# Projecting q, k and v of all heads ahead of a latent attention, with q and k through memory, and spreading another attention's output products over its steps

## The chip, the cores and the metric

The kernel runs on one core of a Trainium2 chip. The metric is the time of one execution on the device in microseconds (us). A core has TensorE (PE in the profile; its weight loads are PEld), VectorE (DVE), ScalarE (ACT), GpSimd (POOL) and SyncE (SP, which issues nearly all DMAs here). They run side by side, each through a queue of its own, and wait for each other by semaphores. A "bank" below is a piece of PSUM, the memory that TensorE writes; it holds 128 rows of 512 floats.

## The reference

One decoder layer on x of 1024 tokens by 1024 features, all in float32:

```
h  = RMSNorm(x);  p = h @ w_in          # q, k, v of local attention | latents of q, kv | rope key | two gates
A  = local attention (8 heads of 64, 2 kv heads, window 128, learned sinks)
B  = latent attention: q = norm(q latent) @ w_uq, 8 heads of 64 + 32 rotary
                       k, v = norm(kv latent) @ w_ukv, 8 heads of 64 each
                       causal softmax over 1024 keys
y  = sigmoid(gate_a) * (A @ w_o_swa) + sigmoid(gate_b) * (B @ w_o_mla)
x  = x + y @ w_out;  x = x + SwiGLU(RMSNorm(x));  out = RMSNorm(x)
```

## The kernel before, in words

Every product is made in three matmuls: each operand is split into a high and a low part (`split`, L161 on: ScalarE copies the high part, VectorE subtracts it for the low one), and `mm3` (L169 on) adds high by high, high by low and low by high in a bank. So each tensor that TensorE is to read costs a ScalarE and a VectorE instruction first.

Order of the stages: the input projections, local attention with the gate products beside it (its outputs go to memory as oa_d), the latent attention, the output products of both attentions, the product with w_out, the feed-forward part, and the final norm. The change lies in the latent attention and in the output products.

*The latent attention.* The normalised latents are transposed into cq (three tiles) and ckv (two). Four helpers project them: `prod_rope(s)` (L1093) makes the rotary parts of q for all heads and 512 tokens and stores them to memory (qr_d), `prod_q(j, s)` (L1108) makes the other 64 rows of q of heads 2j and 2j+1, for 512 tokens, in one unit of 9 matmuls of 128x512, `prod_k(j, s)` (L1124) the same for k in 6, and `prod_v(b)` (L1132) v of all heads for 128 tokens in 6. prod_q and prod_k read their bank out in two halves of 64 rows, one per head, straight into that head's tiles qT and kT; the rotary rows of qT come from qr_d by DMA, and those of the three kT tiles, which are used in turn, are split three times from the transposed rope key.

Then come 64 steps (`for t in range(NT)`, L1301), eight per head, each a block of 128 queries, in the order 2, 3, 6, 7, 0, 1, 4, 5 (L1145). `scores(t)` (L1150) writes a block's scores to scb, one of two double banks; VectorE adds the mask and takes the maximum, ScalarE the exponential, GpSimd divides by the sum. `transposes(t)` (L1177) turns the block of probabilities p by TensorE into banks pTb, which ScalarE and VectorE split into pth and ptl. `pv(h, j)` (L1192) multiplies two blocks with v into half of a bank ob; when its second half is full, ScalarE and VectorE add up the parts. pTb, ob and the products oA come from the same four banks (`P1`, L153).

In step t stand: scores of step t+2; a pv that is due (4 steps behind its second block); in heads 0, 2, 4 a prod_q and in heads 1, 3, 5 a prod_k for the next heads, two of each; in the last eight steps a unit of `mix_a`; the transposes of step t-1; and splits of inputs for what follows.

*The output products.* `mix_a(dc, sh)` (L1248) is a unit of 12 matmuls: 128 columns of A @ w_o_swa for 512 tokens. `mix_b(dc)` (L1346) does the same for B in two units, multiplies both by the gates (loaded by `load_sig`, L1239) and adds. `early` (L1299) puts seven units of mix_a into the last eight steps; one follows behind, and the other eight are mixed with mix_b as listed in `steps` (L1361). The results of the first eight units wait in SBUF tiles ar.

*What sets the order.* Up to the end of local attention the order of PE and SP is the program's own (L329 to L1034). In the latent attention and in the output products it is a planner's: it takes, per engine, the first instruction in the program's order that it expects to be ready by its costs, and a tile waits for a free slot of its pool: 21 slots of 4 KB (`U`, L144), 17 of 8 KB (`V`, L147). Only ScalarE's copies under `held` (L159, L164) keep the program's order. What results is a fixed queue on each engine.

## Time and profile before

| what | value |
|---|---|
| median of 3 executions | 1357.09 us (1356.26 to 1359.11) |
| the profiled execution | 1357.54 us |
| its span in the trace | 1355.8 us, granted clock 0.999 |
| VectorE, ScalarE, GpSimd busy | 67%, 47%, 40% of the span |
| moved by DMA | 206.31 MB, mean 152 GB/s |
| first score matmul of the latent attention | 375.59 us |
| end of its last value product | 556.30 us |

The span starts with the first instruction of the trace and ends with the last. A row of a stretch of time gives its length and each engine's busy time in it, with the number of records. A row of a group or tile gives line, engine, operation, what is written and read, the count and the duration of one in ns (least, median, greatest, in a tile's rows). A row of a wait gives who waited for whom, the total in us, how often, and the longest.

### The profile page before, as it was taken

Reading aid. Unit: us, or ns where it says so; the run is one execution under the profiler, and the core shown is the slowest. Engines: PE = TensorE matmul, PEld = TensorE weight load, DVE = VectorE, ACT = ScalarE, POOL = GpSimd, SP = SyncE. Lnnn points to the kernel's source line nnn. Section 1 sums busy time; section 2 is a strip of 40 time slices with the busy share of each in tenths; the row PEclk is TensorE's granted clock in tenths of the full one; section 3 lists DMA queues with packets and bytes.
Section 4 is the critical chain, followed back from the end, with each engine's and each line's share of the span. In section 5 each row is a group of like instructions: output and inputs, shape, how many; then the busy total and the mean of one; then the engine's idle time right before and its main releaser. Section 6 shows DMA issues by size and latency. Waiting matters only on the chain.

```text
span 1355.8 us, 18965 instructions
## 1 busy us (share of the span) xinstructions
PE 1333.5 (98%) x6564; PEld 1116.0 (82%) x6564; DVE 913.6 (67%) x1493; ACT 641.7 (47%) x1301; POOL 548.9 (40%) x602
## 2 busy tenths in 40 slices
PE   9999999999999999999999999999999999999997
PEld 6899878878788878888887888888888888888886
DVE  7868767776777887585458866666656654664862
ACT  7434666675577777651336232322332332644343
POOL 2116546552254454200031565766665551022521
PEclk9999999999999999999999999999999999999999
DMA  9455322335410111671333353644435425996504
GB/s 372 151 188 163 116 87 82 119 111 190 132 37 16 40 48 32 233 254 42 121 158 140 124 179 143 222 178 179 152 136 179 163 86 184 379 383 242 171 10 146
DMA packets 79840, 206.31 MB, mean 152 GB/s; under 512 B 9089, under 2 KB 15745, under 8 KB 79489
## 3 DMA queue, kind: packets, MB, share of 16 engines
q1 hardware_dynamic: 78304, 202.74, 42.5%
q10 hardware_dynamic: 1440, 2.36, 0.5%
q8 instruction: 52, 0.85, 0.3%
q14 instruction: 44, 0.35, 0.1%
HBM read 143.34 MB, written 61.73 MB: 151 GB/s over the span
## 4 chain that ended last, share of the span: by engine, by line
PE 82%; DVE 7%; ACT 5%; issue 3%; POOL 2%; DMA 1%; ACTq 0%; POOLq 0%; DVEq 0%
PE fa L174 7%; PE fa L172 7%; PE fa L173 7%; PE fb L172 6%; PE fb L174 6%; PE fb L173 6%; PE fd L173 5%; PE fd L174 5%; PE fd L172 5%; PE xo L174 2%; PE xo L172 2%; PE xo L173 2%; DVE ptl L166 1%; DVE scb L1171 1%; ACT p L1172 1%
## 5 line engine op out<-in xcount | busy, mean ns | idle before, releaser
L166 DVE TENSOR_TENSOR wl<-wr,wl 128x512 fp32r<-128x512 f32 x150 | 151.0, 1031 | 72.7 <-ACT wl L163 72.4
L166 DVE TENSOR_TENSOR lrv<-lr,lrv 128x1024 fp32r<-128x1024 f32 x77 | 105.1, 1397 | 49.0 <-ACT lrv L163 46.4
L163 ACT CAST lrv<-lr 128x1024 fp32r<-128x1024 f32 x77 | 80.1, 1052 | 95.3 <-PE fd L174 68.8
L174 PE MATMUL fd<-lrv 128*128 128x512 f32 x308 | 119.9, 389 | 0.0
L172 PE MATMUL fd<-lrv 128*128 128x512 f32 x308 | 119.9, 389 | 0.0
L173 PE MATMUL fd<-lrv 128*128 128x512 f32 x308 | 119.9, 389 | 0.0
L177 POOL TENSOR_TENSOR wr<-wr,sm 128x512 f32<-128x512 f32 (+1 forms) x38 | 46.3, 1227 | 148.3 <-DVE wl L166 116.0
L163 ACT CAST wl<-wr 128x512 fp32r<-128x512 f32 x150 | 86.9, 623 | 2.0 <-DVE wr L826 1.7
L305 POOL TENSOR_SCALAR ms<-ss 128x1 f32<-128x1 f32 x32 | 8.8, 276 | 187.5 <-ACT xn L1578 111.2
L166 DVE TENSOR_TENSOR wl<-sm,wl 128x512 fp32r<-128x512 f32 x60 | 48.6, 835 | 46.6 <-ACT wl L163 46.5
L1173 POOL TENSOR_TENSOR denb<-denb,neg_one 128x1 f32<-128x1 f32 x64 | 36.8, 575 | 87.2 <-ACT p L1172 81.0
L172 PEld LDWEIGHTS fd<-lrv 128*128 128x128 f32 x308 | 57.9, 188 | 12.1
L174 PEld LDWEIGHTS fd<-lrv 128*128 128x128 f32 x308 | 57.9, 188 | 11.9
L173 PEld LDWEIGHTS fd<-lrv 128*128 128x128 f32 x308 | 57.9, 188 | 11.9
L1172 ACT ACTIVATE p<-scb,nmb 128x384 f32<-128x384 f32 (+3 forms) x64 | 47.6, 744 | 33.3 <-DVE nmb L1171 29.4
L166 DVE TENSOR_TENSOR ptl<-pTb,pth 128x512 fp32r<-128x512 f32 (+2 forms) x96 | 49.3, 550 | 19.9 <-ACT pth L163 19.5
L1470 ACT ACTIVATE act<-sm 128x512 f32<-128x512 f32 x11 | 7.0, 633 | 104.9 <-DVE sm L180 104.9
L1171 DVE CUSTOM_DVE_ANT_0 scb<-scb,mask 128x384 f32<-128x384 f32 (+3 forms) x64 | 48.2, 761 | 6.4 <-PE scb L1163 4.3
L1174 POOL TENSOR_SCALAR p<-p,denb 128x384 f32<-128x384 f32 (+3 forms) x64 | 49.5, 774 | 6.3
L1188 PE MATMUL pTb<-ident,p 128*128 128x128 f32 x288 | 44.8, 276 | 3.1 <-DVE ob L1222 1.4
L172 PE MATMUL fa<-t1h,wl 128*128 128x512 f32 x120 | 47.3, 394 | 0.4 <-ACT wl L163 0.4
L172 PE MATMUL fb<-t2h,wl 128*128 128x512 f32 x120 | 47.4, 395 | 0.0
(352 smaller groups left out, 4280.5 us busy)
## 6 DMA issues: line engine op xcount, KB each, us to landing
lr<-la_d SPq DMA_DIRECT2D x77, 256.0 KB, 5.4
wr<-in_w_gate_dram SPq DMA_DIRECT2D x22, 512.0 KB, 4.2
wr<-in_w_up_dram SPq DMA_DIRECT2D x22, 512.0 KB, 5.1
wd<-in_w_down_dram SPq DMA_DIRECT2D x22, 512.0 KB, 6.9
rb_d<-wd SPq DMA_DIRECT2D x22, 512.0 KB, 2.7
la_d<-sd SPq DMA_DIRECT2D x22, 512.0 KB, 5.3
lr<-rb_d SPq DMA_DIRECT2D x44, 256.0 KB, 5.4
lr<-in_w_down_dram SPq DMA_DIRECT2D x33, 256.0 KB, 5.4
```

Source lines behind the costliest of these rows:

```text
L163: i = nc.scalar.copy(hi, src)
L166: (eng or nc.vector).tensor_tensor(lo, src, hi.bitcast(F32), op=ALU.subtract)
L172: nc.tensor.matmul(ps, ah, bh, start=first and i == 0, stop=False, skip_group_check=go_on)
L173: nc.tensor.matmul(ps, ah, bl, start=False, stop=False, skip_group_check=go_on)
L174: nc.tensor.matmul(ps, al, bh, start=False, stop=last and i == n - 1, skip_group_check=go_on)
L177: eng.tensor_tensor(out, a, b, op=ALU.subtract)
L305: nc.gpsimd.tensor_scalar(ms, ss, 1.0 / width, EPS, op0=ALU.mult, op1=ALU.add)
L1171: nc.vector.tensor_tensor_reduce(s_, s_, m_, 1.0, -NEG, op0=ALU.add, op1=ALU.min, accum_out=nm)
L1172: nc.scalar.activation(p_, s_, AF.Exp, scale=-1.0, bias=nm, accum_out=den)
L1173: nc.gpsimd.tensor_tensor(den, den, neg_one[:, 0:1], op=ALU.pow)
L1174: nc.gpsimd.tensor_scalar(p[:, 0:w], p[:, 0:w], den, 0.0, op0=ALU.mult, op1=ALU.add)
L1188: nc.tensor.transpose(pp[:, i], p[:, blk(k0 + i)], ident)
```

## The change

Two new pairs of memory tensors take q and k of all heads (qn_d, kn_d), and a third the products A @ w_o_swa (ar_d).

Ahead of the steps all units of prod_rope, prod_q, prod_k and prod_v now stand in one loop over j, with the first two scores among the last of them. prod_q and prod_k read their bank out whole (128 rows) into a staging tile, which goes to memory; `load_k(h)` and `load_q(h)` bring a head's 64 rows back, three and two heads ahead. The rope key is split once, and two DMAs copy its rows to the other two kT tiles.

In the steps, heads 1 to 7 get four half units of mix_a each, of 6 matmuls: in the second and third step of a head the two halves of one unit, in the sixth and seventh those of another. So 14 units lie in the steps, and two follow. oa's loads stand ahead of the steps, its splits in the first eight. The transposes of step t stand in step t, and a pv is due after 3 steps. The w_o_swa weights are split in heads 0, 2, 4 and 6, into slots of V.

Behind the steps only mix_b is left. The product of mix_a comes back from ar_d with the two gates (`load_sigs`). The gate's product and one of the two additions are on GpSimd.

```
-    for nm, dp in (("oa", 0), ("oa", 1), ("oa", 2), ("ob", 0), ("ob", 1), ("oa", 3), ("ob", 2), ("ob", 3)):
-        plain((nm, dp), (w_o_swa if nm == "oa" else w_o_mla)[dp], (P, 4, 256))
+    for dp in range(4):
+        plain(("oa", dp), w_o_swa[dp], (P, 4, 256), True)
+    for dp in range(4):
+        plain(("ob", dp), w_o_mla[dp], (P, 4, 256))
...
-        for hi, lo in kT:
-            split(hi[64:QK, half(s)], lo[64:QK, half(s)], pr.rearrange("p b c -> p (b c)"))
+        split(kT[0][64:QK, 0, half(s)], kT[0][64:QK, 1, half(s)], pr.rearrange("p b c -> p (b c)"))
+    for i in range(1, 3):
+        nc.sync.dma_start(kT[i][64:QK].bitcast(F32), kT[0][64:QK].bitcast(F32))
...
     def prod_q(j, s):
...
-        for u in range(2):
-            hi, lo = (v[0:64, half(s)] for v in qT[2 * j + u])
-            p = ps[64 * u:64 * u + 64]
-            nc.scalar.activation(hi, p, AF.Copy, scale=-SC_B)
-            nc.vector.scalar_tensor_tensor(lo, p, -SC_B, hi.bitcast(F32), op0=ALU.mult, op1=ALU.subtract)
+        t = U("qns", F32R, (P, 2, 512))
+        nc.scalar.activation(t[:, 0], ps, AF.Copy, scale=-SC_B)
+        nc.vector.scalar_tensor_tensor(t[:, 1], ps, -SC_B, t[:, 0].bitcast(F32), op0=ALU.mult, op1=ALU.subtract)
+        nc.sync.dma_start(qn_d[j][:, :, half(s)], t.bitcast(F32))
...
     def prod_k(j, s):
...
-        for u in range(2):
-            hi, lo = kT[(2 * j + u) % 3]
-            split(hi[0:64, half(s)], lo[0:64, half(s)], ps[64 * u:64 * u + 64])
+        t = U("kns", F32R, (P, 2, 512))
+        split(t[:, 0], t[:, 1], ps)
+        nc.sync.dma_start(kn_d[j][:, :, half(s)], t.bitcast(F32))
...
+    def load_k(h):
+        nc.sync.dma_start(kT[h % 3][0:64].bitcast(F32), kn_d[h // 2, 64 * (h % 2):64 * (h % 2) + 64])
+
+    def load_q(h):
+        t = qT[h] = V("qT", F32R, (P, 2, S))
+        nc.sync.dma_start(t[0:64].bitcast(F32), qn_d[h // 2, 64 * (h % 2):64 * (h % 2) + 64])
+        for i in range(2):
+            nc.sync.dma_start(t[64 + 16 * i:80 + 16 * i].bitcast(F32), qr_d[i, 16 * h:16 * h + 16])
...
+    def mix_a(dc, sh, c0, n, ps=None):
...
+        mm3(ps, [((w[0][:, c, blk(dc % 2)], w[1][:, c, blk(dc % 2)]), oaT[(c, sh)]) for c in range(c0, c0 + n)],
+            c0 == 0, c0 + n == 4)
+        if c0 + n == 4:
+            nc.scalar.copy(ar[dc][:, half(sh)], oa_ps.pop((dc, sh)))
+            if sh == 1:
+                nc.sync.dma_start(ar_d[dc], ar.pop(dc))
...
+    def load_sigs(dc):
+        for i in (dc, 8 + dc):
+            load_sig(i)
+        ar[dc] = U("ar")
+        nc.sync.dma_start(ar[dc], ar_d[dc])
+
+    for j in range(4):
+        prod_k(j, 0)
+        prod_k(j, 1)
+        if j < 2:
+            prod_rope(j)
...
+        prod_q(j, 0)
+        if j == 1:
+            load_k(0)
+        if j == 2:
+            load_k(1)
+            load_q(0)
+        if j == 3:
+            load_k(2)
+            load_q(1)
+            psum_phase("psb", 2)
+            scores(0)
+        prod_q(j, 1)
+        prod_v(2 * j)
+        if j == 3:
+            scores(1)
+        prod_v(2 * j + 1)
+        if j == 1:
+            for g in range(2):
+                load_oa(g, 0)
+        if j == 3:
+            for g in range(2):
+                load_oa(g, 1)
+    st.load_to(st.index[("oa", 0)])
+    fill = {}
+    for i in range(16 - 2):
+        for c in range(2):
+            fill[NB * (i // 2 + 1) + 4 * (i % 2) + 1 + c] = (i // 2, i % 2, 2 * c)
...
-        if h + 1 < NH:
-            if n in (2, 4) and h % 2 == 0 and h + 2 < NH:
-                prod_q(h // 2 + 1, n // 2 - 1)
-            if n in (3, 5) and h % 2 == 1:
-                prod_k((h + 1) // 2, n // 2 - 1)
+        if n == 2 and h + 2 < NH:
+            load_q(h + 2)
+        if n == 6 and h + 3 < NH:
+            load_k(h + 3)
...
-            pvq.append((t + 4, hh, nn // 2))
+            pvq.append((t + 3, hh, nn // 2))
...
-        if e in early:
-            mix_a(*early[e], (PX if e >= 6 else P1)("oA"))
-        if t:
-            transposes(t - 1)
+        if t in fill:
+            dc, sh, c0 = fill[t]
+            mix_a(dc, sh, c0, 2, P1("oA") if c0 == 0 else None)
+        transposes(t)
...
+        if t < 8:
+            split_oa(t % 4 // 2, t // 4, t % 2)
+        if t == 4:
+            st.conv_to(st.index[("oa", 0)])
+        if n in (0, 4) and h in (2, 4, 6):
+            (st.load_to if n == 0 else st.conv_to)(st.index[("oa", h // 2)])
+        if e == 4:
+            load_sigs(0)
...
+    rest = [(i // 2, i % 2) for i in range(14, 16)]
+    mix_a(*rest[0], 0, 4, PX("oA"))
     for _, hp, j in pvq:
         pv(hp, j)
+    for r in rest[1:]:
+        mix_a(*r, 0, 4, PX("oA"))
...
     def mix_b(dc):
...
+        a_ = ar.pop(dc)
+        for sh in range(2):
+            nc.gpsimd.tensor_tensor(ga[:, half(sh)], a_[:, half(sh)], ga[:, half(sh)], op=ALU.mult)
...
+        for sh in range(2):
+            cs = half(sh)
+            add(ga[:, cs], ga[:, cs], gb[:, cs], (nc.vector, nc.gpsimd)[sh * (dc < 7)])
             split(*hT(dc, cs), ga[:, cs])
...
+    for dc in range(8):
+        if dc + 2 < 8:
+            load_sigs(dc + 2)
+        if dc % 2 == 0 and dc < 6:
+            st.load_to(st.index[("ob", dc // 2 + 1)])
+        if dc + 1 < 8:
+            sigmoids(dc + 1)
+        mix_b(dc)
+        if dc % 2 == 1 and dc < 6:
+            st.conv_to(st.index[("ob", dc // 2 + 1)])
+        if dc >= 4:
+            st.load_to(st.index[("out", 0, dc - 4)])
+        if dc >= 5:
+            st.conv_to(st.index[("out", 0, dc - 5)])
```

123 lines of the change are left out of this document (24 added, 99 removed).

## The prediction

> **What bounds the kernel now.** I read the page first, for the engine that sets the end, and then the latent attention by itself, because every part of the change lies in it or touches it.
>
> ```profile
> span 1355.8 us, 18965 instructions
> ...
> PE 1333.5 (98%) x6564; PEld 1116.0 (82%) x6564; DVE 913.6 (67%) x1493; ACT 641.7 (47%) x1301; POOL 548.9 (40%) x602
> ...
> PE 82%; DVE 7%; ACT 5%; issue 3%; POOL 2%; DMA 1%; ACTq 0%; POOLq 0%; DVEq 0%
> ```
>
> TensorE is busy 98% of the span and carries 82% of the chain of waits. The change moves matmuls without adding or dropping one, so it can only win time in which TensorE is not fed, and lose by starving it elsewhere. Busy time overstates feeding, because matmul records overlap. I therefore count starts. The next fence has the stretches of time from the first score matmul of each head to that of the next, the last stretch cut at 544; then the end of the attention, the projections ahead of it, and the output products behind it. Columns: length, then busy time (records) of PE, PEld, DVE, ACT, POOL, granted clock, DMA share, GB/s.
>
> ```profile
> 375.59:391.30 15.71, 15.15 (x87) 12.57 (x86) 11.80 (x25) 10.28 (x24) 8.35 (x14) 1.00 0.13 38
> 391.30:411.30 20.00, 19.12 (x127) 16.57 (x126) 17.00 (x37) 15.36 (x36) 10.05 (x15) 1.00 0.13 28
> 411.30:432.55 21.25, 20.37 (x133) 17.77 (x131) 16.26 (x36) 15.80 (x36) 11.69 (x18) 1.00 0.02 3
> 432.55:453.25 20.70, 19.25 (x125) 16.43 (x125) 15.80 (x35) 13.61 (x32) 9.11 (x15) 1.00 0.11 26
> 453.25:474.27 21.02, 20.10 (x133) 17.66 (x131) 16.65 (x36) 16.40 (x38) 11.48 (x18) 1.00 0.15 49
> 474.27:495.02 20.75, 19.38 (x126) 16.46 (x125) 17.42 (x38) 15.03 (x35) 9.72 (x15) 1.00 0.16 51
> 495.02:514.76 19.74, 18.14 (x118) 14.79 (x116) 17.90 (x36) 16.64 (x37) 10.85 (x16) 1.00 0.09 29
> 514.76:544.00 29.24, 29.04 (x169) 25.03 (x169) 19.53 (x41) 19.23 (x42) 13.09 (x18) 1.00 0.17 51
> 544.00:556.30 12.30, 12.30 (x76) 10.38 (x74) 5.58 (x9) 6.32 (x14) 1.46 (x2) 1.00 0.21 74
> ...
> 348.40:375.59 27.19, 26.46 (x114) 20.68 (x113) 18.60 (x30) 12.66 (x23) 10.07 (x8) 1.00 0.45 127
> 556.30:640.00 83.70, 83.70 (x372) 69.31 (x371) 55.22 (x72) 40.19 (x49) 10.01 (x4) 1.00 0.53 198
> ```
>
> The last row gives the full rate: 372 matmuls of 512 columns in 83.70 us, 0.225 each, nothing lost. Narrower ones are read in the timeline of TensorE (start, length, name):
>
> ```profile
> 388.72 1.04 PE L1188 MATMUL pTb<-ident,p 128*128 128x128 f32 x8
> 389.51 0.48 PE L1162 MATMUL scb<-kT,qT 96*128 96x512 f32 x1
> ...
> 390.42 0.28 PE L1210 MATMUL ob<-pth,vM 128*128 128x256 f32 x1
> 390.54 0.28 PE L1211 MATMUL ob<-ptl,vM 128*128 128x256 f32 x1
> ```
>
> A transpose takes 0.10 (0.79 over 8), a 256-column matmul 0.12. By the code a head has 36 score matmuls, 15 of them of 512 columns (15 x 0.225 = 3.4; the 21 narrower ones, scaled between 0.12 and 0.225, 2.95), 36 transposes (3.6) and 40 value products (32 x 0.117 + 8 x 0.06 = 4.2): 14.15 us. What a head takes beyond this and beyond its filling matmuls is lost. Heads 2 and 4 hold 18 matmuls of prod_q (4.05 us), heads 1, 3 and 5 hold 12 of prod_k (2.7), head 6 none. Lost in heads 1 to 6: 3.15, 3.05, 3.85, 2.8, 3.9, 5.6. Head 0 loses 1.75 (its 87 records at these rates come to 13.95); from 514.76 to 556.30 lie 18.85 us of attention and 89 products oA (20.0), so 2.7 is lost in 41.5, or 0.065 per us. Together **26.8 us**, the most that the change could win. The pattern is what I argue from: the more independent matmuls beside a head, and the lower VectorE's share (0.91 in head 6, 0.67 from 514.76), the smaller the loss. The waits of TensorE between 376 and 515 say what it waits for:
>
> ```profile
> PE scb L1161 <- ACT p L1172: 2.3, 6, 0.8
> PE pTb L1188 <- DVE ob L1222: 1.4, 6, 0.3
> PE ob L1210 <- DVE ptl L166: 1.4, 4, 0.4
> PE pTb L1188 <- DVE ptl L166: 1.2, 4, 0.5
> ```
>
> All are ends of a chain through VectorE or ScalarE: a bank not yet read out (first, second and fourth row), a probability not yet split (third).
>
> **The change part by part.** Durations of what is moved:
>
> ```profile
> L1122 DVE SCALAR_TENSOR_TENSOR qT<-q,qT x16: 682/688/693, 370.0 to 474.6; 64x512 fp32r<-64x512 f32 x16
> ...
> L166 DVE TENSOR_TENSOR kT<-k,kT x16: 671/688/693, 365.9 to 497.6; 64x512 fp32r<-64x512 f32 x16
> ...
> L166 DVE TENSOR_TENSOR wv<-oar,wv x8: 677/684/1284, 471.1 to 514.8; 128x512 fp32r<-128x512 f32 x8
> ...
> L166 DVE TENSOR_TENSOR wl<-wr,wh x4: 1218/1225/1226, 509.8 to 550.4; 128x1024 fp32r<-128x1024 f32 x4
> ...
> L1257 ACT COPY ar<-oA x8: 585/586/593, 523.2 to 558.4; 128x512 f32<-128x512 f32 x8
> ```
>
> *Heads 1 to 5.* Six prod_q and six prod_k leave the steps, and with them four VectorE instructions per head, 4 x 0.688 = 2.75 us of a mean 16.6. Some four split_oa (4 x 0.684, heads 4 and 5) leave too, a mean of 0.55; an output weight's split (1.23 in heads 2, 4 and 6) comes, 0.5. VectorE falls to 16.6 - 2.75 - 0.55 + 0.5 = 13.8 us per head. In come four half units of mix_a, 24 matmuls, 5.4 us, and only two ScalarE copies of 0.586. With 14.15 + 5.4 + 1.9 = 21.45 us VectorE's share is 0.64, below the 0.67 of the best stretch. Its rate, 0.065, would give 1.4 lost; heads 2 and 4, with a little less filling and much more VectorE work, lose 2.9. I take 1.9, nearer the row with the same VectorE share: 9.5 us for five heads, where they lost 16.75.
>
> *Heads 6 and 7.* The same filling, plus three split_ob each and a weight split: I take 2.5 and, with the end of the attention, 3.2, where 8.3 was lost.
>
> *Head 0.* It loses its filling and takes eight split_oa (six in this stretch: 6 x 0.684 = 4.1) and a weight split (1.23). VectorE: 11.8 - 2.75 (prod_q) - 1.4 (two prod_v) + 4.1 + 1.23 + 2.1 (the readout of the last three projections) = 15.1. At 0.91, the highest share above, that needs 16.6 us; TensorE has 9.45 of attention and 21 projection matmuls, 4.7, so VectorE alone would make it lose 2.5. I take 3.0, between 1.75 as now and head 6's 5.6.
>
> *Transposes and values one step earlier.* The transposes of a step now stand in that step, so the probability has two steps instead of three to be made:
>
> ```profile
> L1173 POOL TENSOR_TENSOR denb<-denb,neg_one 128x1 f32<-128x1 f32 x64 | 36.8, 575 | 87.2 <-ACT p L1172 81.0
> ...
> L1172 ACT ACTIVATE p<-scb,nmb 128x384 f32<-128x384 f32 (+3 forms) x64 | 47.6, 744 | 33.3 <-DVE nmb L1171 29.4
> ...
> L1171 DVE CUSTOM_DVE_ANT_0 scb<-scb,mask 128x384 f32<-128x384 f32 (+3 forms) x64 | 48.2, 761 | 6.4 <-PE scb L1163 4.3
> L1174 POOL TENSOR_SCALAR p<-p,denb 128x384 f32<-128x384 f32 (+3 forms) x64 | 49.5, 774 | 6.3
> ```
>
> That chain is 0.76 + 0.74 + 0.58 + 0.77 = 2.85 us; two steps are 5.4 us with filling and some 4.3 in head 0. I cost it at nothing; the cover is the filling, and without it one wait of 0.5 (the longest on ptl above) per step would be 4 us a head, which is about what head 6 loses now.
>
> Sum of the steps: 3.0 + 9.5 + 2.5 + 3.2 = 18.2 against 26.8: **-8.6 us**.
>
> *Projections ahead.* Some 90 matmuls (20.3 us) come here from the steps. The stretch from 348.40 has 114 matmuls, 25.7 us at full rate, and loses 1.5, so 0.055 per us: **+1.1**. VectorE has 24 readouts of 0.69 for 24 units of 1.35 or 2.03 us, and four of the six krT splits fall away. New are stores of 512 KB, reloads of 64 rows, and the first head's wait for both. The nearest rows:
>
> ```profile
> qr_d<-qrs SPq DMA_DIRECT2D x4, 512.0 KB, 3.2
> qT<-qr_d SPq DMA_DIRECT2D x16, 128.0 KB, 3.4
> ...
> sg<-gate_d SPq DMA_DIRECT2D x11, 512.0 KB, 6.6
> ```
>
> ```profile
> L166 POOL TENSOR_TENSOR qrs<-qr,qrs x4: 1283/1300/1302, 357.8 to 365.3; 128x512 fp32r<-128x512 f32 x4
> ```
>
> A store and a load are 3.2 + 3.4 = 6.6 us, up to 10 behind other traffic. load_k(0) stands a group of projections behind its stores, load_q(0) more than 9 us of matmuls ahead of scores(0); the tightest is qr_d, whose second half leaves GpSimd after a sum, a difference and two splits, 4 x 1.3 = 5.2 us, while 21 us of matmuls (five prod_q, four prod_v, four prod_k) stand between its last product and scores(0). I count nothing for the wait; uncovered it costs up to 6.6, and the four krT splits saved could give back 1. What SP holds up behind a waiting reload is stores, and through them the staging tiles of prod_q and prod_k: one comes every 1.9 us and is held 0.6 + 0.7 + 3.2 = 4.5, so two or three of the 21 slots. Later reloads have one to two heads, 20 to 40 us. [...] No run here shows a 64-row load yet.
>
> *Output products behind.* mix_a's last 8 units leave this stretch, with no gain or loss by themselves: it is at the full rate. What remains is 8 mix_b of 5.4 us. Each needs three 512 KB tiles (the product comes back from memory) instead of 2, so some 14.7 MB (seven such triples, three ob and four out weights) must arrive in about 46 us, 320 GB/s. Rows for what is possible:
>
> ```profile
> 560.00:565.00 5.00, 5.00 (x24) 4.14 (x23) 1.66 (x3) 4.99 (x6) 2.05 (x1) 1.00 1.02 410
> 595.00:600.00 5.00, 5.00 (x24) 4.14 (x23) 1.99 (x4) 0.00 (x0) 0.00 (x0) 1.00 1.00 370
> ```
>
> At 370 to 410 GB/s it takes 36 to 40 us, so it fits with two units' lead; at dc 4 and 5 a unit asks 2.1 MB in 5.4 us, about 390, which is the edge. I take **+1**, bounds 0 and +6. VectorE there has per dc two products, one addition and two splits (5 x 0.69 = 3.45, at the rows' 0.69 for 512 columns) and at most 1.8 of weight splits (1.23 for an out, half of one for an ob), 5.3 of 5.4; GpSimd two products and an addition at the 1.3 above, 3.9. [...]
>
> Sum: -8.6 + 1.1 + 1.0 = -6.5; 1357.5 (the profiled execution, whose span is 1355.8; the median of the three runs is 0.4 lower) gives **1351.0 us**. With the heads all at 0.065 and head 0 as now it is 1343.
>
> **The rivals.**
> 1. *The filling fills nothing.* TensorE takes its queue in order; if the half units stand beside other work and not in the gaps, heads 1 to 7 lose the 3 of heads 1 and 2 and only head 6's excess goes: 7 x 3 + 3.0 = 24 against 26.8, -2.8 + 1.1 + 1.0 = -0.7, or 1356.8. For it: prod_q's 4.05 us bought only 0.8 over prod_k's 2.7. Against: the stretch from 514.76.
> 2. *Slower: the product's bank.* A unit split over two steps keeps one of ps1's four banks from its first half to the copy behind its second, 4 us; an ob pair holds another for two steps; transposes get two. Waits of pTb now are up to 0.5. If each of the 28 halves adds 0.35, that is +10: 1361. It decides from the point where a bank's transposes, copy and split (0.4 + 0.6 + 0.6 and two handovers) take longer than TensorE's work between two groups, in the wide steps (n of 6, 7, 4, 5), two of which the fills fall on.
> 3. *Transfers bind.* Ahead, about 18 MB (8.4 of q and k, 2.1 of rope, reloads, oa) fall into 47 us, 385 GB/s, and behind 320. At the 370 row both ends run late: 3 + 5 us on the forecast, 1359.
>
> **How the numbers follow.** The measurement tells 0.2%, 2.7 us, from no change. The forecast has 0.54, all of it faster; rival 1 has 0.18 (0.14 same, 0.04 faster), the bank 0.18, all slower, the transfers 0.10 (0.04 same, 0.06 slower). Faster 0.58, same 0.18, slower 0.24. The forecast's own range is 1343 to 1354; with the rivals' prices 1343 to 1362 leaves some 2 in 10 out, mostly above.
>
> **What would show it.** Right: TensorE's rows in heads 1 to 5 near 136 records in 21.5 us, VectorE near 0.64, no wait of scb on p; a full-rate row behind the attention. Wrong: head 0 beyond 19 us; waits of pTb on ptl or ob longer than now; TensorE idle on a DMA at the first scb or at oB; heads as long as 23 us with the same work.

## The result, and the profile after

| | before | after |
|---|---|---|
| median of 4 runs each on one chip | 1358.10 us (1356.26 to 1359.46) | 1367.30 us (1365.05 to 1370.91) |
| the profiled execution | 1357.54 us | 1365.05 us |
| its span, granted clock | 1355.8 us, 0.999 | 1363.2 us, 0.991 |

The changed kernel takes 1.0071 times as long, 95% interval 1.0042 to 1.0100: slower by 9 us, where 6.5 less was forecast and 1362 was the upper end. The page of the changed kernel:

```profile
span 1363.2 us, 19047 instructions
...
PE 1332.9 (98%) x6564; PEld 1120.6 (82%) x6564; DVE 898.6 (66%) x1458; ACT 634.7 (47%) x1289; POOL 577.9 (42%) x621
...
PE 86%; DVE 4%; issue 3%; POOL 3%; ACT 2%; DMA 1%; POOLq 0%; ACTq 0%; DVEq 0%
```

TensorE's work is the same and the span is 7.4 us longer. The stretches of time by head, with the columns of the prediction's second fence (the first is the projections, the last ends with the last value product):

```profile
343.58:394.87 51.29, 50.32 (x225) 41.09 (x224) 25.41 (x41) 15.81 (x29) 10.17 (x8) 1.00 0.82 266
394.87:413.42 18.55, 15.77 (x86) 13.89 (x86) 15.31 (x31) 12.91 (x30) 9.06 (x14) 0.82 1.01 304
413.42:433.39 19.97, 17.92 (x116) 15.54 (x116) 16.14 (x35) 14.88 (x36) 12.24 (x16) 1.00 0.47 103
433.39:454.02 20.63, 20.63 (x139) 18.69 (x138) 13.20 (x30) 13.82 (x33) 10.16 (x16) 1.00 0.28 83
...
515.92:536.56 20.64, 20.64 (x140) 18.71 (x138) 13.18 (x30) 14.01 (x33) 10.29 (x16) 1.00 0.15 53
536.56:568.02 31.46, 30.87 (x202) 27.50 (x201) 23.18 (x43) 24.11 (x52) 16.78 (x21) 1.00 0.32 117
```

Heads 2 to 6 are fed without a break: five times 20.63 us, VectorE at 0.64 to 0.71. Head 0 isn't: 86 records in 18.55 us, where the kernel before had 87 in 15.71, and its granted clock is 0.82. TensorE's losses are counted as in the prediction, from start to start less the work at its rates, but with the matmuls that the trace has in each stretch, for both kernels (so the column of before differs a little, by row, from the prediction's; its sum is the same 26.8). A plus sign means more than before:

| stretch | before | forecast | after |
|---|---|---|---|
| projections, from the rope key's transposes | 1.9 | +1.1 | 1.9 |
| head 0 | 1.9 | 3.0 | **7.2** |
| heads 1 to 5 | 16.6 | 9.5 | 7.3 (3.55, then four times 0.8 to 1.1) |
| head 6 | 5.2 | 2.5 | 1.1 |
| head 7 to the last value product | 3.1 | 3.2 | 2.8 |
| from there to 690 us | 1.6 | +1 | **18.1** |

The steps as a whole won 8.4 us (26.8 to 18.4), where 8.6 were forecast. The stage behind them lost 16.5 more than before, and that is the result. Its stretches:

```profile
570.00:575.00 5.00, 5.00 (x23) 4.13 (x23) 3.19 (x6) 2.59 (x4) 0.00 (x0) 1.00 0.63 204
575.00:580.00 5.00, 5.00 (x23) 4.13 (x22) 2.62 (x4) 3.16 (x4) 3.23 (x3) 1.00 1.02 406
580.00:585.00 5.00, 1.30 (x6) 0.75 (x4) 3.03 (x5) 2.15 (x4) 3.68 (x3) 0.92 1.02 411
585.00:590.00 5.00, 2.77 (x6) 1.76 (x7) 3.32 (x2) 4.21 (x6) 4.99 (x4) 0.50 1.03 411
590.00:595.00 5.00, 5.00 (x15) 3.91 (x14) 1.38 (x2) 1.10 (x2) 3.28 (x3) 0.55 1.02 409
595.00:600.00 5.00, 5.00 (x24) 4.14 (x23) 2.03 (x4) 1.61 (x3) 1.28 (x1) 1.00 1.03 410
...
615.00:620.00 5.00, 2.74 (x7) 1.92 (x8) 4.96 (x7) 2.99 (x4) 1.55 (x2) 0.84 0.78 270
```

TensorE's timeline at the first gap, and its waits from 545 to 690:

```profile
580.92 0.39 PE L174 MATMUL oB<-obT,wl 128*128 128x512 f32 x1
586.04 0.79 PE L172 MATMUL oB<-obT,wh 128*128 128x512 f32 x1 [4.74 <-ACT wh L163]
586.63 0.63 PE L173 MATMUL oB<-obT,wh 128*128 128x512 f32 x1
```

```profile
PE oB L172 <- ACT wh L163: 4.7, 1, 4.7
PE xo L172 <- ACT wv L163: 2.2, 1, 2.2
PE xo L173 <- DVE wv L166: 1.7, 1, 1.7
PE oB L174 <- DVE wl L166: 1.3, 2, 1.2
```

All that it waits for in the output products is weights that ScalarE and VectorE haven't split. Two costs follow from one gap: the gap itself, and then the clock. TensorE is idle from 581 to 586, and until 594 its matmuls start 0.43 us apart, not 0.225 (15 records in 590 to 595, 24 in 595 to 600). ScalarE's and VectorE's own rows, and SP's, show four suspects: SP stood at the stores of the last two products, 11.5 us at the first and 6.9 at the second, until 571, while the transfers ran at 137 to 183 GB/s; then they ran full at 410; ScalarE's queue has the copies of y, which wait for additions, ahead of the weights' splits; and VectorE's and GpSimd's instructions take longer than the prediction's rows had them.

```profile
SPq L1267 <- ACT ar L1265: 18.3, 2, 11.5
```

```profile
ACT yh L163 <- DVE sg L180: 17.3, 8, 3.9
ACT yh L163 <- POOL sg L180: 14.2, 7, 3.4
```

```profile
L166 DVE TENSOR_TENSOR yl<-sg,yh 128x512 fp32r<-128x512 f32 x16 | 15.3, 963 | 12.2 <-ACT yh L163 11.8
...
L166 DVE TENSOR_TENSOR wl<-wr,wh 128x1024 fp32r<-128x1024 f32 x4 | 7.0, 1762 | 1.9 <-ACT wh L163 1.9
```

```profile
L1374 POOL TENSOR_TENSOR sg<-ar,sg 128x512 f32<-128x512 f32 x14 | 22.9, 1659 | 4.7 <-ACT sg L1248 4.3 <-DMA ar<-ar_d 0.4
L180 POOL TENSOR_TENSOR sg<-sg,sg 128x512 f32<-128x512 f32 x7 | 10.9, 1560 | 23.4 <-DVE sg L1379 22.1 <-ACT yh L163 1.3
```

### The profile page after: what moved, and what is told of

It is laid out like the page before. It is cut to its first block, busy times and chain, and to the rows that moved or that the text cites. A ratio compares the mean times of both kernels' runs of the same rounds, so it can differ in the third digit from the quotient of the medians.

```text
span 1363.2 us, 19047 instructions
## 1 busy us (share of the span) xinstructions
PE 1332.9 (98%) x6564; PEld 1120.6 (82%) x6564; DVE 898.6 (66%) x1458; ACT 634.7 (47%) x1289; POOL 577.9 (42%) x621
## 4 chain that ended last, share of the span: by engine, by line
PE 86%; DVE 4%; issue 3%; POOL 3%; ACT 2%; DMA 1%; POOLq 0%; ACTq 0%; DVEq 0%
PE fa L174 7%; PE fa L172 7%; PE fa L173 7%; PE fb L174 6%; PE fb L172 6%; PE fb L173 6%; PE fd L172 5%; PE fd L174 5%; PE fd L173 5%; PE xo L173 2%; PE xo L174 2%; PE pTb L1192 2%; PE xo L172 2%; PE ob L1215 1%; PE ob L1214 1%
## 5 line engine op out<-in xcount | busy, mean ns | idle before, releaser
L172 PE MATMUL xo<-wv,yh 128*128 128x512 f32 x120 | 47.4, 395 | 2.2 <-ACT wv L163 2.2
L173 PE MATMUL xo<-wv,yh 128*128 128x512 f32 x120 | 46.8, 390 | 1.7 <-DVE wv L166 1.7
L1192 PE MATMUL pTb<-ident,p 128*128 128x128 f32 x288 | 43.8, 279 | 3.9 <-POOL p L1178 3.8
```

Of the source, the lines that this page charges most:

```text
L172: nc.tensor.matmul(ps, ah, bh, start=first and i == 0, stop=False, skip_group_check=go_on)
L173: nc.tensor.matmul(ps, ah, bl, start=False, stop=False, skip_group_check=go_on)
L1192: nc.tensor.transpose(pp[:, i], p[:, blk(k0 + i)], ident)
```

## Experiments on the output stage

Totals of single executions don't decide here: up to the rope key's transposes, where the program is the same in all, executions already differ by up to 6 us (343.5 to 349.4 us), and head 1 by as much (below). (Each kernel of this section ran once. Only the joint kernel, 1363.51 us, and the one without GpSimd's products, 1361.84, came out under the changed kernel's lowest time, and neither computes the whole layer.) So the measure is the stage itself: from the start of the first latent product matmul (oB) to that of the first transpose of the feed-forward part, 336 matmuls, 75.6 us at 0.225 each, and **92.9** in the changed kernel, 17.3 more.

**The last store away.**

```
-            if sh == 1:
+            if sh == 1 and dc < 7:
                 nc.sync.dma_start(ar_d[dc], ar.pop(dc))
...
-        ar[dc] = U("ar")
-        nc.sync.dma_start(ar[dc], ar_d[dc])
+        if dc < 7:
+            ar[dc] = U("ar")
+            nc.sync.dma_start(ar[dc], ar_d[dc])
```

> The changed kernel with one thing undone: the last product (dc 7) stays in SBUF, neither stored nor reloaded. Watched: the 192 matmuls oB, 43.2 us at full rate, which take 60.7 from first to last start in the changed kernel (570.3 to 631.0), so 17.5 lost, and the row of waits in which SP is held 6.9 us by ScalarE's copy of that last product. Theory Q (the order of the queue: SP stands behind that store while the DMA engines are idle, and all later loads start 7 us late): oB takes 45 to 52 us, the span falls by 8 to 14 from 1363.2. Theory B (the bytes: three tiles per unit are too many for 410 GB/s whatever their order): 1 MB of 15 less is 2.6 us, so oB takes 57 to 59 and the span falls by 2 to 4.

The stage took 92.2 us (1366.32 for the run), 0.7 less: the 6.9 us that SP stood at this store weren't the cause by themselves; the wait of oB on wh grew to 8.4. The longer hold, 11.4 at the store of the product before, stayed in this run.

**No reads.** Each gate is multiplied by the other gate instead of the product.

```
-        nc.sync.dma_start(ar[dc], ar_d[dc])
...
-            nc.gpsimd.tensor_tensor(ga[:, half(sh)], a_[:, half(sh)], ga[:, half(sh)], op=ALU.mult)
+            nc.gpsimd.tensor_tensor(ga[:, half(sh)], gb[:, half(sh)], ga[:, half(sh)], op=ALU.mult)
```

> The changed kernel without the reload of the products from memory (8 x 512 KB); the stores stay. It leaves out the first attention's product in the gated sum: the gate is multiplied by the other gate's tile instead. Theory B (bytes): 4.2 MB less, 10 us of transfer, oB takes 43 to 46 us and the span falls to 1347 to 1350. Theory Q (order): SP is still held 6.9 us by the last store and the weights still stand behind gate tiles, now 4 instead of 7, so oB still takes 48 to 55.

The 192 oB matmuls came 5.2 us closer (55.4 from first to last start, from 60.6), the stage only 2.6 (90.4). With 4.2 MB less, bytes are at most a small part.

**The weights of the latent products earlier.**

```
+    st.load_to(st.index[("ob", 1)])
     load_sigs(1)
...
+        if dc % 2 == 1 and dc < 6:
+            st.conv_to(st.index[("ob", dc // 2 + 1)])
+            st.load_to(st.index[("ob", min(dc // 2 + 2, 3))])
...
```

> The changed kernel with the same bytes, but the w_o_mla weights loaded ahead of the gate tiles of the same turn and split before the unit ahead of their use, not behind it. Theory Q, in the form that the weights' place in the queues is what TensorE waits for: the wait of oB on the weight's split (4.7 + 1.3 us) and the half clock behind it go, oB takes 44 to 50 us. If the late start of SP is the larger part, gate tiles come late instead and oB takes 52 to 58. Theory B: the same 58 to 61.

92.5 us. oB gained 3.8, and the product with w_out, which comes next, lost it.

**Idle matmuls in the gaps**, of results that nobody reads:

```
+        if dc in (2, 6):
+            idle = P1("idle")
+            for i in range(24 if dc == 2 else 16):
+                nc.tensor.matmul(idle, obT[(0, 0)][0][:, 0:P], obT[(0, 0)][0], start=True, stop=True)
```

> The changed kernel with 40 more matmuls of 512 columns (9.0 us at full rate) into an unused bank, 24 ahead of unit dc 2 and 16 ahead of dc 6, where TensorE stands idle. If the granted clock of 0.50 (584 to 594, and 0.83 near 618) follows TensorE's own idleness, the clock stays at 1.0 there, the matmuls behind the stall run at 0.225 instead of 0.43, and the span falls by 2 to 5 us though 9 us of work are added. If the clock falls for another reason (the DMA traffic, say), it still falls and the span is the same or up to 4 us longer.

With 40 matmuls (9 us) more the stage took 3.3 us **less**, 89.6. It begins 9.6 us later in this run, so 595 to 605 here is what 585 to 595 was there:

```profile
595.00:600.00 5.00, 5.00 (x24) 4.02 (x23) 3.12 (x2) 3.64 (x4) 4.99 (x4) 1.00 1.03 413
600.00:610.00 10.00, 10.00 (x46) 8.29 (x45) 6.80 (x10) 4.46 (x6) 5.02 (x5) 1.00 1.03 409
610.00:620.00 10.00, 8.39 (x38) 6.61 (x37) 7.21 (x7) 4.72 (x7) 8.34 (x6) 1.00 1.03 410
```

The clock stays at 1.00 while the transfers are as full as before, so the halved clock followed TensorE's own idleness. It is worth at least the 3.3 us that this run won net of its added work.

**The second addition on VectorE again.**

```
-            add(ga[:, cs], ga[:, cs], gb[:, cs], (nc.vector, nc.gpsimd)[sh * (dc < 7)])
+            add(ga[:, cs], ga[:, cs], gb[:, cs], nc.vector)
```

> The changed kernel with the second addition of mix_b back on VectorE, as it was before the change, and nothing else. None of the three runs that gave SP an earlier start, fewer bytes or the weights first brought oB under 55 us; in all of them ScalarE's queue stands 1 to 5 us at a time at the split of a sum that GpSimd adds, and the next weight's split is queued behind it. Theory G (GpSimd's addition at the head of ScalarE's queue): oB takes 44 to 50 us (60.7 in the changed kernel), the waits of oB on the weight's split fall under 2 us. Theory B (the bytes): 57 to 61. VectorE has 6 x 0.69 + at most 1.8 = 5.9 us per dc of 5.4, so 1 to 3 us late at the end by its own work.

91.4 us, 1.5 less: not the cause by itself either.

So four edits buy 0.4 to 2.6 each. The next runs put them together. **Store and weights** is the first and the third; **joint** has the reads away too (each gate is multiplied by the other gate in the product's place).

> The changed kernel with two edits together: the last product stays in SBUF (no store, no read of it) and the weights of the latent products are loaded and split earlier; the other seven products are read back as in the changed kernel, so this is the joint kernel with its reads put back. Theory 'reads' (seven reads of 0.5 MB at some 410 GB/s are 9 us of transfers that nothing covers): from the first to the last latent product matmul 55 to 58 us, 7 to 10 over the joint kernel's 48.2. Rival 'order' (with the store and the weights out of the way the reads fit): 48 to 51.

> The changed kernel with three edits at once that were tried one by one: the products are not read back (each gate is multiplied by the other gate in the product's place, but for the last, which stays in SBUF), the last product isn't stored, and the weights of the latent products are loaded and split earlier. Theory 'joint' (late loads, bytes and the late weight split each suffice to stop TensorE, so that taking one away shows the next): from the first to the last of the 192 latent product matmuls 44 to 48 us (60.6 changed, 55.4 without the reads alone), and the run 9 to 14 us under the changed kernel's 1367. Rival 'chain' (the sigmoids, products, additions and splits of ScalarE, GpSimd and VectorE in a row set the pace): still 53 us or more.

Store and weights: stage 86.5, oB 53.6. Joint: stage 87.4, oB 48.2. Together the two edits buy 6.4 us where they bought 1.1 apart: with one of them the other still stops TensorE. By oB alone the reads look worth 5.5 us, and my theory seemed to hold; but the next product gave all of it back (xo lost 6.6 where it lost 0.3), waiting for the splits of y. The joint run is only 3.8 us under the changed kernel, not 9 to 14: the theory fell, and the chain of the other engines was left, or a late start of the loads, for SP still stood at the store of the last product but one until 571 in the one and 568 in the other.

**Early loads.** The last two products stay in SBUF, the gates come a block earlier, and the weights as in "store and weights".

```
-            if sh == 1:
+            if sh == 1 and dc < 6:
...
-        if e == 4:
-            load_sigs(0)
+        if e == 1:
+            load_sigs(0)
+        if e == 4:
+            load_sigs(1)
+        if e == 5:
+            st.load_to(st.index[("ob", 1)])
...
```

> The changed kernel with the last two products kept in SBUF (their stores, for which SP stood until 571 us while the transfers were nearly idle, are gone), the gates and products of the first two column blocks loaded three and four steps before the end, those of the others three blocks ahead instead of two, and the weights earlier as in 'store and weights'. Theory 'late start' (the transfers of the output stage begin only when SP has let the last store go, and never catch up): from the first latent product matmul to the first transpose of the feed-forward part, 336 matmuls and 75.6 us at full rate, 78 to 82 us where the changed kernel takes 92.9 and 'store and weights' 86.5. Rival 'chain' (the copies of y wait in ScalarE's queue for the additions, and the weights' splits stand behind them): 85 to 88.

> The kernel 'early loads' without the reads of the first six products: each of those gates is multiplied by the other gate instead, so 3 MB less is moved. Theory 'late start' with room in the transfers: the same as 'early loads' within 1.5 us. Rival 'reads' (bytes bind even with an early start): 3 us or more less than 'early loads'.

86.6 and 86.6 us: the gates of the first two blocks and two weights are now issued before 564, ahead of the stage's start at 578, and it is no shorter than with store and weights; without the reads nothing changes. So the hold at the last stores isn't the rest of the cause. The loads of the third block still begin only at 575, after a wait of 11.2 us. SP's waits in "early loads" name what it waits for now, slots that GpSimd holds:

```profile
SPq L1245 <- POOL sg L1379: 16.3, 3, 11.2
SPq L1245 <- POOL sg L180: 10.6, 3, 4.4
```

**GpSimd's products away**, on top of "early, no reads":

```
-        for sh in range(2):
+        for sh in range(2 * (dc >= 6)):
             nc.gpsimd.tensor_tensor(ga[:, half(sh)], a_[:, half(sh)], ga[:, half(sh)], op=ALU.mult)
```

> The kernel 'early, no reads' without the gate's product on GpSimd for the first six column blocks (the sigmoid is added as it is), so that GpSimd keeps its additions and the last two products, some 20 of its 34 us of work here are gone, and ScalarE's, VectorE's and TensorE's instructions stay. Theory 'GpSimd' (its products of 1.66 us make the additions late, hold the slots that the loads wait for, and stretch VectorE's splits to 0.96 and 1.76 us where they took 0.69 and 1.23 before): the 336 matmuls from the first latent product to the first transpose of the feed-forward part take 77 to 81 us instead of 86.6, and VectorE's splits of y come down to 0.7 to 0.8 us. Rival 'ScalarE and VectorE' (their own work and order set the pace): 84 to 87.

81.3 us, 5.3 less, just beyond the 77 to 81 of the theory and well below the rival's 84 to 87, which fell. Counted from the start of the stage, the third block's gates and the third weight are issued within 0.6 us of where they were without this edit, so earlier loads hardly explain the gain. oB is at the full rate (43.8 us from first to last). VectorE's and GpSimd's rows:

```profile
L166 DVE TENSOR_TENSOR yl<-sg,yh 128x512 fp32r<-128x512 f32 x16 | 13.2, 831 | 9.1 <-ACT yh L163 8.6
```

```profile
L1376 POOL TENSOR_TENSOR sg<-ar,sg 128x512 f32<-128x512 f32 x4 | 6.0, 1516 | 3.5 <-ACT sg L1248 3.5
```

The split of y takes 0.83 us on the mean, between 0.96 in the changed kernel and 0.69 before, where GpSimd was busy 10 us in this stage; the 0.7 to 0.8 that was expected it did not reach, and the additions on GpSimd remain. This edit takes a link out of the chain ahead of the additions and also shortens VectorE's splits; no run parts the two.

The 17.3 us, as far as these runs take them apart: 6.4 for the last store and the weights' place together, 5.3 for GpSimd's products, none for the reads, and 5.7 that no run removed, 4.9 of them lost in the product with w_out, with waits on the copies of y. The halved clock (3.3 us or more) is inside these, not beside them.

One thing the stage alone hides: the early loads cost time in head 7. From head 7's first score to the same transpose the changed kernel takes 126.6 us, store and weights 120.2, early loads 123.2, without the reads 125.7, and without GpSimd's products 118.0. So early loads are worth nothing over store and weights, and the last kernel wins 8.6 us over the changed one, not the stage's 11.6.

## Experiments on the first heads

**Projections ahead alone**: the kernel before, with the projections ahead of the steps and through memory, and the output products as before.

> The kernel before with one part of the change alone: q, k and v of all heads projected ahead, q and k through memory; the output products stay where they were (seven units in head 7, eight between mix_b's), so heads 1 to 6 have no filling matmuls. Theory F (filling decides what a head loses): each of heads 1 to 6 loses 4.5 to 6 us, as head 6 did in the kernel before (5.3), 18 to 20.5 us long, against 2.9 to 3.9 before. Rival V (VectorE's relief by the larger readouts decides): heads 1 to 6 lose 2 or less. Both: the output products behind the attention stay at full rate, 0 to 1 us lost. By F the span is 1364 to 1370, by V 1349 to 1354.

1362.43 us, between the two theories. Heads 2 to 6, now without any filling, lose 3.2 to 5.0 each, much as before with it, and head 0 7.1. So relieving VectorE about made up for the filling that left, and the products brought the loss down to 1 (not the earlier transposes: the mixed kernel below, which leaves them where they were, loses 1.1 to 1.3 in the two heads that have products and little else). The output stage is at the full rate, and head 0's loss doesn't come from the spreading, nor from the earlier transposes, which this kernel doesn't have.

**The last projections into head 0; the first weight earlier; the first pair directly.** In the third, q and k of heads 0 and 1 are split straight into their tiles. The three edits, one after the other, the first and the last cut to their core:

```
+    first = {0: (prod_v, 6), 1: (prod_v, 7), 2: (prod_k, 3, 0), 3: (prod_k, 3, 1), 4: (prod_q, 3, 0), 6: (prod_q, 3, 1)}
...
         if j == 1:
+            st.load_to(st.index[("oa", 0)])
             load_k(0)
...
+        if j == 0:
+            for u in range(2):
+                split(kT[u][0:64, 0, half(s)], kT[u][0:64, 1, half(s)], ps[64 * u:64 * u + 64])
+            return
```

> The changed kernel with the last group of projections (two prod_v, two prod_k, two prod_q, 42 matmuls, 9.5 us) moved from ahead of the steps into head 0's, and the splits of the local attention's output four steps later. In the changed kernel and the three runs after it head 0 lost 5.4 to 7.2 us and head 1 3.6 to 10.1, and the first scores waited 2 for qT. If head 0 lacks filling (F), heads 0 and 1 together lose 3 to 6. If late transfers are the larger cause (ScalarE stood 3.4 us for the first output weight, issued 15 us earlier, in a stretch where the DMA engines were busy all the time), they lose 8 or more still. The output products behind lose the same 16 to 18.

> The changed kernel with the first w_o_swa weight loaded a group of projections earlier, and nothing else. If ScalarE's wait for that load is what makes head 1 long (10.1 us lost in one run, where it waited 3.4, and 3.6 in another), head 1 loses 3 to 4 and no wait of ScalarE on it is seen; head 0 is the same. If head 1's loss is the lack of filling, it is as long as in the other runs, 5 to 10.

> The changed kernel with q and k of heads 0 and 1 split straight into their tiles, as before, and the rope products first; only the other three pairs go through memory. Theory 'reload' (head 0 loses 7.2 us because its q arrives late and the transfers ahead of it fill the queues): head 0 loses 2 to 4. Rival 'filling' (it has no products left between its scores): 6 to 8 as now, and only the wait for q ahead of the first score, 0.9 us, goes. The output stage stays at about 60 us.

In the first, heads 0 and 1 lose 6.5 and 3.2, together more than the 8 that was to speak for late transfers, and TensorE stood ahead of the first score:

```profile
PE scb L1165 <- DMA qT<-qr_d: 9.2, 1, 9.2
```

In the changed kernel the same wait is 0.9, because those projections cover it: the reload of head 0's q is as late as that. With the weight earlier (it landed at 384.8, and ScalarE didn't wait for it) heads 0 and 1 lose 6.1 and 6.8. With the first pair directly they lose 5.0 and 7.0, between the 2 to 4 and the 6 to 8 of the two theories: the late q isn't the whole, though the projections slid into head 0, where they stood in a block ahead of its steps and not between them.

**The splits moved** to head 1, and the first products to head 2, on top of "the first pair directly":

```
-        if t < 8:
-            split_oa(t % 4 // 2, t // 4, t % 2)
+        if 8 <= t < 16:
+            split_oa(t % 4 // 2, t // 4 - 2, t % 2)
...
```

> The kernel 'direct first' with the eight splits of the local attention's output moved from head 0 to head 1 and the first two output products moved from head 1 to the end, so that head 0 keeps the projections that slid into it and loses the splits, and head 1 has the splits and no products. Theory 'splits' (eight splits of 0.5 to 1 us each on ScalarE and VectorE ahead of the scores' own work make p late): head 0 loses 1.5 to 3 where it lost 5.0, and head 1 keeps 6 or more. Rival 'filling': head 0 stays at 4.5 to 6 and head 1 loses 4 to 5 as in 'ahead only'.

Head 0 lost 6.3, head 1, with the splits and no products, 3.85: the splits aren't the cause. Head 2, which now has the first products, lost 6.3. In heads 0 and 2 the granted clock was 0.88 and 0.85, in head 1 1.00.

**Idle matmuls in head 0**, two a step:

```
+    oaT0 = vM[0].rearrange("p h d -> p (h d)")[:, 0:512]
...
+        if t < 8:
+            idle = P1("idle")
+            for i in range(2):
+                nc.tensor.matmul(idle, oaT0[:, 0:P], oaT0, start=True, stop=True)
         transposes(t)
```

> The changed kernel with two matmuls of 512 columns, whose result nobody reads, ahead of the transposes in each of head 0's eight steps: 16 of them, 3.6 us of work that the output doesn't need. Theory 'clock' (of the 7.2 us that head 0 loses, 3.3 are the granted clock, halved after gaps of 1 to 2 us, and the rest is the gaps themselves): the clock stays at 1.00, the idle work lies in the gaps, and head 0 takes 15.5 to 17 us, less than its 18.55 with 3.6 us of work more. Rival 'chain' (head 0's length is set by the chain through VectorE, ScalarE and GpSimd alone, and the clock only slows work that would have waited): 18.5 to 19.5 us. Second rival (the idle work adds to it): 21 or more.

Head 0 took 15.44 us with ten of them in it, at a clock of 1.00: the halved clock that was in its 18.55 is gone. The 3.1 us less overstate it, though: the stretch holds 8 value products where the changed kernel's holds 24, and the other 16, 1.9 us, slid into head 1. So 1.2 us are won, with 2.25 us of idle work in the stretch, and the 15.5 to 17 of the clock theory were met only by that shift (17.3 with them; the chain theory had 18.5 to 19.5). Head 1 then took 28.1 us. ScalarE's longest wait, and the stretches:

```profile
ACT wv L163 <- DMA wr<-in_w_o_swa_dram: 4.4, 1, 4.4
```

```profile
410.00:415.00 5.00, 5.00 (x34) 4.37 (x34) 2.97 (x7) 1.80 (x5) 2.05 (x2) 1.00 1.07 237
415.00:420.00 5.00, 0.79 (x6) 0.47 (x4) 2.43 (x5) 2.01 (x4) 0.00 (x0) 1.00 1.02 225
420.00:425.00 5.00, 4.60 (x13) 3.43 (x14) 3.03 (x8) 2.97 (x7) 2.55 (x4) 0.50 0.71 177
```

The first weight of w_o_swa was issued at 402.4 and landed some 14 us later, behind the stores and reloads of q and k; ScalarE's queue is fixed, so the copies of the next probabilities stood behind it, and TensorE behind those. In the changed kernel's profiled execution the weight landed after 12.3 us, just as ScalarE came to it. In nine of the ten other kernels whose text is the changed kernel's up to head 7, ScalarE waited 0.9 to 3.5 us for it, and in all ten head 1 lost 5.4 to 10.0 instead of 3.55. So the profiled execution, the fastest of the four, is a lucky one here, and the spread of the changed kernel's times (5.9 us, 3.2 before) is probably this; that link is argued. The late weight isn't the whole of head 1's loss either: with the weight earlier nobody waited for it and head 1 lost 6.8, with a mean clock of 0.87 from 413 to 440 us. In the changed kernel's profiled execution the halved clock fell into head 0 (403.3 to 410.2), and head 1 kept 1.00. What decides this stays open.

## A kernel that keeps the gain

If the filling is right and the stage behind is what fails, the filling should come from elsewhere: q and k of pairs 1 to 3 as whole 128-row splits through memory in the steps of heads 0 to 3, two output products a head in heads 4 to 7, and the output stage left as it was.

```
+    prods = {0: (prod_k, 1, 0), 1: (prod_k, 1, 1), 4: (prod_q, 1, 0), 5: (prod_q, 1, 1),
+             9: (prod_k, 2, 0), 10: (prod_k, 2, 1), 13: (prod_q, 2, 0), 16: (prod_q, 2, 1),
+             19: (prod_k, 3, 0), 21: (prod_k, 3, 1), 25: (prod_q, 3, 0), 28: (prod_q, 3, 1)}
...
+    for i in range(7):
+        for c in range(2):
+            early[NB * (i // 2 + 4) + 4 * (i % 2) + 1 + c] = (i // 2, i % 2, 2 * c)
```

> The kernel before with the filling spread and nothing else moved: the first pair of heads projected as before straight into its tiles; q and k of the other three pairs projected in the steps of heads 0 to 3 as whole 128-row splits and taken through memory; seven of local attention's output products, two to a head, in the steps of heads 4 to 7; the output stage as before, with products of both kinds taking turns and no product through memory. Theory of the tail (the step's gain is real, the separated output stage gives it back): heads 1 to 6 lose 1 to 2 us each where before loses 2.9 to 5.2, head 0 loses 2 to 3, head 7 about 3, the output stage stays at full rate, so the time is 1345 to 1350. Rival (filling in the steps is worth little where not the projections too are moved ahead): heads lose 3 or more and the time is 1354 to 1360.

1358.03 us, 1.0005 times before (0.9995 to 1.0014): no difference. Heads 0 to 3 lost 1.6 to 2.7, heads 5 and 6 1.3 and 1.1; but head 4 lost 5.3, head 7 6.3 and the output stage 6.1. The theory for the stage: its loads were issued when they always were, and the stage came 7 us earlier. The second version issues them earlier, and spreads the splits of local attention's output over heads 3 to 5:

```
+        if e in (1, 3):
+            first_gates[e // 2] = V("sgv", F32, (P, 2, 1024))
+        if 1 <= e < 5:
+            load_sig((4, 0, 8, 1)[e - 1])
+        if e == 2:
+            st.load_to(st.index[("oa", 2)])
...
```

> The mixed kernel (seven output products in heads 4 to 7, the rest beside the latent products as before) with the loads of the output stage issued about 10 us earlier: four gates go into free slots of the large pool, and the first two weights are loaded in head 7; the splits of local attention's output are spread over heads 3 to 5. Theory 'loads' (moving 7 us of TensorE work out of head 7 brought the output stage 7 us nearer, and its loads didn't move): head 4 loses 2 instead of 5.3, head 7 3 to 4 instead of 6.3, the output stage 1.5 to 3 instead of 6.1, so the time is 1348 to 1352. Rival: the stalls stay or move, 1355 to 1359.

**1354.38 us, 0.9962 times before (0.9948 to 0.9976)**: faster than both kernels, by 4 and 13 us. The stretches of heads 4 to 7 and of the output stage:

```profile
459.03:483.01 23.98, 22.66 (x134) 19.17 (x133) 18.97 (x39) 16.54 (x36) 10.49 (x15) 0.93 0.59 153
483.01:503.93 20.92, 20.86 (x138) 18.73 (x137) 15.93 (x35) 15.28 (x36) 11.26 (x18) 1.00 0.34 78
503.93:524.56 20.63, 20.63 (x139) 18.71 (x137) 14.78 (x31) 14.72 (x34) 11.04 (x17) 1.00 0.15 52
524.56:559.95 35.39, 31.79 (x201) 27.26 (x199) 25.29 (x45) 30.12 (x57) 15.75 (x21) 1.00 0.35 121
559.95:620.00 60.05, 60.05 (x268) 49.74 (x268) 45.31 (x61) 30.49 (x38) 6.61 (x3) 1.00 0.61 219
```

The stage behind the attention is full again (1.6 lost to 690, as in the kernel before). Head 4, with the splits of local attention's output and a clock of 0.93, and head 7, with ScalarE at 0.85, still lose 5.7 and 6.9, so the theory's 1348 to 1352 wasn't reached, and half of it failed.

## Why the prediction was wrong

- **The step that failed** is "Output products behind. (...) I take +1, bounds 0 and +6". It was 16.5, beyond its bound; all other terms together came out within 1 us of their sum. The step looked at bytes (14.7 MB, 320 GB/s: they moved at 410, and did not bind in the end) and at each engine's sum against the 5.4 us of a block. The sums were about right: from the first to the last oB of the changed kernel VectorE was busy 4.9 us a block, where the prediction had at most 5.3, GpSimd 4.2, where it had 3.9, and ScalarE 3.9. No run shows the +1 itself: TensorE waited for no DMA in this stage, and its four waits, 9.9 us, are on splits of weights. What failed is reading a sum under 5.4 as no loss. These engines wait for each other in a chain through fixed queues (the copies of y wait 31.5 us for additions, and the weights' splits stand behind them), and in that chain instructions were longer than the prediction had them: GpSimd's 1.56 to 1.66 us and not 1.3, VectorE's splits 0.96 and 1.76 and not 0.69 and 1.23.
- What had kept this stage at the full rate, by my reading, was the eight units of mix_a in it, 21.6 us of TensorE work in which the gates, sums and splits got done. "With no gain or loss by themselves" is where the text went wrong: those units were cover. Both kernels that keep them there (projections ahead alone, the second mixed one) are at the full rate; but they also read nothing back and leave GpSimd less to do (10 us busy in before's stage), and no run gave the changed kernel its units back alone, so this part is argued.
- "It fits with two units' lead" took the loads to start in time. SP stood at the stores of the last two products, 11.5 and 6.9 us. The second of these holds away bought 0.7, with the weights' place 6.4.
- Head 0, 3.0 against 7.2: the gaps and the half clock of an unfilled head weren't priced. TensorE waited there for p (1.8 for the transposes, 0.9 for the scores), and 6.8 us of it ran at half the clock. The prediction had named the danger: "the cover is the filling, and without it one wait of 0.5 (...) per step would be 4 us a head"; but it cost it "at nothing", though head 0 has no filling left. That the earlier transposes are what cost it isn't shown: projections ahead alone leaves them where they were, and loses 7.1.
- The steps' sum of -8.6 came out (-8.4), and that is luck: head 0 lost 4.2 more than forecast, heads 1 to 6 3.6 less and head 7 0.4 less, and head 1's loss in this execution is the smallest of the eleven kernels with the same text up to there. The mechanism in heads 2 to 6 was right, and better than forecast: VectorE's share was 0.64 to 0.71, and the loss per us 0.05, below the 0.065 row.
- Rival 1 (the filling fills nothing) fell: heads 2 to 6 lose 1, not 3. Rival 2 (the product's bank) fell: no wait of pTb on a bank in these heads. Rival 3 (transfers bind) named both places, ahead and behind, but with the wrong price behind and the wrong reason there; ahead, its 3 us did not come (the projections lose 1.9, as before, where +1.1 was forecast), and the full transfers show behind them instead, in the late first weight.
- The 64-row reloads, which no run had shown then, ran at 217 GB/s where whole stores of 128 rows ran at 410, about half: two rows of the changed kernel, the first with stores of k, the second with the reload of one head's k, DMA engines full in both.

```profile
396.00:398.00 2.00, 1.28 (x6) 0.82 (x5) 1.53 (x5) 1.67 (x5) 0.83 (x2) 1.00 1.06 410
...
416.00:418.00 2.00, 0.34 (x3) 0.34 (x4) 2.00 (x6) 1.20 (x3) 1.90 (x3) 1.00 1.05 217
```

The reload that fills the second row, 512 KB from 415.8 to 418.3, took 2.5 us. The prediction gave the later reloads 20 to 40 us and counted nothing for them; but such reloads stood in front of the weight that ScalarE needed.

## What to carry to other kernels

Matmuls that stand beside other engines' work can be cover for it: before moving them, add up, per block, what each of the other engines has to do in the time that is left, at the durations that they have when all run at once (here 0.96 us for a split of y, not 0.69), and follow the chain between them. A load is hidden only if it is issued early enough for the new place of its reader; when TensorE work moves, move the loads with it (with earlier loads the second mixed kernel lost 1.6 us in the output stage, the first 6.1). And price a gap of TensorE twice: the gap, and the half clock behind it (here 4.7 us, and then a clock of 0.50 for 8.4 us more).

## What the runs showed of the hardware

- The granted clock fell to 0.50 with TensorE partly busy. In head 2 of the kernel with the splits moved (columns as above), one gap of 1.28 us, which ended at 436.1, came before it:

```profile
434.00:435.00 1.00, 0.79 (x3) 0.47 (x3) 0.60 (x2) 1.00 (x3) 0.84 (x2) 1.00 1.18 295
435.00:436.00 1.00, 0.00 (x0) 0.00 (x0) 1.00 (x4) 1.00 (x2) 1.00 (x1) 1.00 1.07 213
436.00:437.00 1.00, 0.90 (x7) 0.86 (x8) 1.00 (x1) 1.00 (x4) 0.47 (x2) 1.00 0.90 180
437.00:438.00 1.00, 0.69 (x3) 0.13 (x1) 1.00 (x4) 0.98 (x4) 0.90 (x2) 0.64 1.07 213
```

  It fell at 437.3, with eight transposes and matmuls just behind TensorE, which by its records was busy 2.0 of the 3.4 us before, and stayed at 0.50 to 444.1. In the output stage of the changed kernel it fell 2.9 us into the gap of 4.7, with TensorE busy 0.5 of the 3.4 us before, and stayed to 594.5. The changed kernel's stretches at 0.50 up to 700 us are 403.3 to 410.2, 584.2 to 594.5 and 618.4 to 621.8, so 6.8, 10.2 and 3.4 us long. What sets when the clock falls and for how long isn't shown by these runs.
- Some of VectorE's splits took longer beside GpSimd. The splits of y in the changed kernel (duration least, median, greatest in ns), and in the kernel before (mean 690):

```profile
L166 DVE TENSOR_TENSOR yl<-sg,yh x16: 681/693/1782, 576.5 to 635.5; 128x512 fp32r<-128x512 f32 x16
```

```profile
L166 DVE TENSOR_TENSOR yl<-sg,yh 128x512 fp32r<-128x512 f32 x16 | 11.0, 690 | 5.4 <-ACT yh L163 5.0
```

  In the changed kernel seven of the sixteen ran beside no GpSimd instruction, and all seven took 0.69 us; the six that took 0.96 to 1.78 each ran beside one (three more did so without being longer). The product of a bank with a gate (L1379), which reads one operand from SBUF where the split reads two, took 0.68 to 0.69 all sixteen times, also beside GpSimd. With GpSimd's products away the mean of the splits of y fell from 0.91 to 0.83, though four weight splits of 128x1024 rose from 1.31 to 1.44 in the same pair of runs. What makes a split longer beside GpSimd isn't shown by these runs.
